# A hybrid decoder layer (gated linear attention and RWKV-7): one burst over four PSUM banks instead of two bursts over two

## The chip, the cores and the metric

The kernel runs on one core of one Trainium2 chip. The metric is device time in microseconds of one execution, the median of several. TensorE is written PE, VectorE DVE, ScalarE ACT, GpSimd POOL and SyncE, which starts the DMAs, SP.

## The reference

One layer is applied to 1024 prompt tokens and to 8 single sample tokens, in float32. The input is projected by `w_in` (1024 rows) to the columns of three groups: gated linear attention (GLA, 4 heads), RWKV-7 (16 heads of 64), and two gates. Both branches are recurrences over the tokens. The RWKV-7 one is, per head,

```python
def step(S, inp):
    rt, wt, kt, vt, kkt, at = inp
    sa = jnp.einsum('bhvk,bhk->bhv', S, -kkt)
    S = S * wt[:, :, None, :] + sa[..., None] * (kkt * at)[:, :, None, :] + vt[..., None] * kt[:, :, None, :]
    y = jnp.einsum('bhvk,bhk->bhv', S, rt)
    return S, y
...
m = (jax.nn.sigmoid(gate_a) * jnp.einsum('btc,cd->btd', o_gla, w_up_gla)
     + jax.nn.sigmoid(gate_b) * jnp.einsum('btc,cd->btd', o_rwkv, w_up_rwkv))
out = jnp.einsum('btd,de->bte', m, w_out)
y_out = _layernorm(DEEPNORM_ALPHA * x + out, ln_g, ln_b, LN_EPS)
```

The outputs are the layer's result for both groups of tokens and the new states.

## The kernel before

The prompt is worked on in two passes of 512 tokens (`PASS`, contexts `c` with `c.i` 0 and 1); the 8 sample tokens ride with the first. Everything is held with the channel on the 128 partitions and the token along the row. A weight block of 128 columns is projected by 24 matmuls a token tile (8 blocks of rows, and three products of high and low parts), in `blocks`; the two banks of tag `proj` take the results.

The RWKV-7 heads are worked on two at a time, head 0 on partitions 0 to 63 and head 1 on 64 to 127 (`HS`). So there are 8 pairs a pass, 16 in all; below they are counted 0 to 15 in order of time. A pair goes through these steps, each a generator that yields its instructions:

- `front`: decays and normalised keys; then the chunk matrices. The 512 tokens are `NCH` = 8 chunks of `C` = 64. The tile `BK` holds, for each chunk, the b and the k columns side by side (for head 1 in the order k, b: the slice begins at `h * C`), `AZ` the vectors that they are multiplied with. Two bursts of matmuls, for chunks 0 to 3 and 4 to 7, each over two PSUM banks (one a head), are masked by two multiplies each into `GG`. The diagonal blocks of `GG` go to DRAM (`LD`) and back, and 31 steps on DVE invert them (tile `X`, of which there is one buffer); the result goes over DRAM (`XD`) into `XT`.
- `back`: the off-diagonal blocks of the inverse.
- `turn`: transposes of the b and k rows of `BK` (16 transposes over two banks, copied back over `BK` itself), and of v.
- `chain`: the recurrence over the 8 chunks, three small matmuls each, one pair after the other (`self.chained`), in the bank of tag `pch`, with the outputs summed in the bank `pY`.
- `norm`: the norm over each head, bonus and gate.

The four GLA heads of a pass (`gla_head`), the low-rank projection (`low_rank`), the sample tokens and the loading of weights are further streams. PSUM has eight banks: 2 `proj`, 4 `big`, 1 `pch`, 1 `pY`. `BK`, `AZ`, `GG` and the tile `wide` have two buffers each, so two pairs are under way at most; rows of 512 or 520 tokens share 33 buffers (`row`).

The order of instructions is not written out. `Order.run` holds one pending instruction per stream, estimates when each could start, from costs and due times in the source, and issues the one with the earliest start less its stream's priority; the chip's engines then run their queues in that order. Buffers are given out in the same way: a stream that asks for `n` buffers of a tag goes on as soon as at least `n` are free, whoever else is waiting:

```python
        idle = self.idle[tag]
        if keep:
            yield lambda: len(idle) >= n + max(keep, self.wait[tag])
        elif len(idle) < n:
            self.wait[tag] += n
            yield lambda: len(idle) >= n
            self.wait[tag] -= n
```

`together` makes one entry of several PE instructions, so that nothing comes between them. `tr` is a transpose by the identity. `self.C.copy` is a copy on ACT or DVE, whichever is estimated to end first.

Of the kernel before, what the change touches and what calls it, by code (L numbers as in the profile page):

```python
# [20 lines left out]
P = 128  # L21
# [5 lines left out]
HT = TP // 2  # L27
# [5 lines left out]
C = 64  # L33
NCH = HT // C
# [54 lines left out]
HS = (slice(0, 64), slice(64, 128))  # L89
# [142 lines left out]
def together(ops):  # L232

    op = ops[0]
    fns = [x.fn for x in ops]
    op.ways = [(op.eng, lambda: [fn() for fn in fns], sum(x.cost for x in ops))]
    op.ins = [y for x in ops for y in x.ins]
    op.outs = [x.out for x in ops]
    op.eng, op.fn, op.cost = op.ways[0]
    return op  # L240
# [178 lines left out]
class Kern(Order):  # L419
# [679 lines left out]
    def front(self, c, p, st, d):  # L1099
        a, A, V, E = self.a, self.A, self.V, self.E  # L1100
        BK_, L_ = (yield from self.get("bk")), (yield from self.get("wide"))
        az, gg = (yield from self.get("az")), (yield from self.get("gg"))
        BK = BK_.rearrange("p (c t) -> p c t", c=NCH)
# [28 lines left out]
        ps = yield from self.head_sums(te)  # L1132
# [21 lines left out]
        ps = yield from self.head_sums(te)  # L1154
# [7 lines left out]
        H = NCH // 2  # L1162
        mk = self.cst("gmask").rearrange("p (k h t) -> p k h t", k=2, h=2)
        for x in range(0, NCH, H):
            ps = yield from self.get("big", 2)
            ps = [y.rearrange("p (c k t) -> p c k t", c=H, k=2) for y in ps]
            yield together([self.P.matmul(ps[h][:, n], BK[hs, x + n, h * C:h * C + P], AZ[hs, x + n], start=True, stop=True)
                            for n in range(H) for h, hs in enumerate(HS)])
            for h in range(2):
                yield V.tensor_mul(GG[:, x:x + H, :, h], ps[h], mk[:, :, h].unsqueeze(1).to_broadcast([P, H, 2, C]))  # L1170
            self.free(*ps)

        NU = 4 * NCH
        LD = self.dr.tile([4, NCH, 32, 32], F32, name=f"LD{c.i}{p}")
# [28 lines left out]
        H = NCH // 2  # L1203
# [4 lines left out]
        for q in range(2):  # L1208
            b = slice(32 * q, 32 * q + 32)
            for h in range(2):  # L1210
                n = 2 * q + h
# [31 lines left out]

    def turn(self, d):

        bt = d.BK.rearrange("p c t -> p (c t)")[:, :2 * HT].rearrange("p (c h k) -> p c h k", c=NCH, h=2)
        pt = yield from self.get("big", 2)
        yield together([self.tr(pt[h][:, x * C:x * C + C], d.BK[hs, x, h * C:h * C + P])
                        for x in range(NCH) for h, hs in enumerate(HS)])
        for h in range(2):  # L1250
            yield self.C.copy(bt[:, :, h], pt[h].rearrange("p (c k) -> p c k", k=C))
        self.free(*pt)
        d.bt = bt.rearrange("p c h k -> p c (h k)")
        d.u = d.L.rearrange("p (c h v) -> p c h v", c=NCH, h=2)
        pt = yield from self.bank("big", [P, 4, P])
        for n in range(4):
            yield self.tr(pt[:, n], d.v[:, n * P:(n + 1) * P])
        self.free(d.v)
        for h in range(2):
            for n, hs in enumerate(HS):  # L1260
                yield self.C.copy(d.u[HS[1 - h], n::2, h], pt[hs, :, h * C:h * C + C])
        self.free(pt)
# [534 lines left out]
```

## Time and profile before

| what | value |
|---|---|
| median of three runs | 1495.95 us (1495.26 to 1499.39) |
| the profiled execution, its own time | 1493.88 us |
| its span, first to last instruction | 1492.1 us |
| PE busy | 1466.4 us, 98% of the span |
| DVE busy | 1201.9 us, 81% |
| ACT busy | 880.1 us, 59% |
| granted TensorE clock, mean | 0.998 |

In the views a row names the engine, the operation, the tile written and the tiles read (`big<-az,bk`: a bank of tag big from `AZ` and `BK`), and the shape. For PE, `64*128` is the weights' rows and columns, the shape in which the array is used. A matmul of float32 operands is two instructions, a transpose one. The end of a matmul is modelled, and matmuls overlap, so what one costs is the step from its start to the next start, not its duration. All instructions stand at line 219, where the recorded calls are made, so that tiles tell more than lines.

### The profile page before, as it was taken

What the parts mean: (1) busy time and instruction counts of PE and PEld (TensorE: products, weight loads), DVE (VectorE), ACT (ScalarE), POOL (GpSimd) and SP (SyncE); (2) the same over time, 40 slices, a digit from 0 to 9 for tenths busy, and PEclk for the clock granted to TensorE, in tenths of its full rate; (3) what the DMA queues carried; (4) which work ended last, traced back from release to release, by engine and by line L of the source; (5) the groups of instructions that cost most, each with busy time, mean ns of one, the idle gap of its engine ahead of it and who ended that gap; (6) DMA issues with size and microseconds to landing.
All of it is one profiled execution on the core that took longest, in us unless ns stands there. A gap on an engine that the chain in (4) does not pass through costs nothing.

```text
span 1492.1 us, 30560 instructions
## 1 busy us (share of the span) xinstructions
PE 1466.4 (98%) x10678; PEld 1282.5 (86%) x10678; DVE 1201.9 (81%) x3159; ACT 880.1 (59%) x2221; POOL 115.5 (8%) x217
## 2 busy tenths in 40 slices
PE   9999999999999999999999999999999999999997
PEld 6998999999999999787877887787788899988786
DVE  6697889988998898979887998888777876756665
ACT  6665767767677677565754556465646746644210
POOL 1001002101120002001001010101000000000000
PEclk9999999999999999999999999999999999999999
DMA  9876697668767877675566565656554768887432
GB/s 310 282 267 207 221 314 227 218 220 302 234 220 221 297 239 241 185 237 168 165 203 175 161 199 180 181 154 171 177 172 135 234 197 258 282 300 264 143 106 85
DMA packets 211253, 319.01 MB, mean 214 GB/s; under 512 B 91683, under 2 KB 107180, under 8 KB 211100
## 3 DMA queue, kind: packets, MB, share of 16 engines
q1 hardware_dynamic: 211100, 317.06, 66.6%
q8 instruction: 85, 1.39, 0.4%
q14 instruction: 68, 0.56, 0.1%
HBM read 197.32 MB, written 118.61 MB: 212 GB/s over the span
## 4 chain that ended last, share of the span: by engine, by line
PE 83%; DVE 7%; DMA 4%; ACT 2%; issue 1%; SPq 1%; POOL 0%; POOLq 0%; DVEq 0%; ACTq 0%
PE proj L219 51%; PE big L219 22%; PE pch L219 6%; PE pY L219 5%; DVE row L219 2%; SPq L219 1%; DMA row<-o_rwkv 1%; ACT row L219 1%; DMA wraw<-w_in 1%; DVE X L219 1%; DVE wpart L219 1%; DMA wide<-LD 1%; DMA row<-state_rwkv 1%; DVE Xt L219 0%; ACT L397 0%
## 5 line engine op out<-in xcount | busy, mean ns | idle before, releaser
L219 PE MATMUL proj<-xs,wpart 128*128 128x264 f32 (+2 forms) x5640 | 1028.6, 327 | 1.2 <-DVE row L219 0.8
L219 PEld LDWEIGHTS proj<-xs,wpart 128*128 128x128 f32 x5640 | 814.4, 189 | 80.8 <-issue 10.3
L219 ACT CAST wpart<-wraw 128x512 fp32r<-128x512 f32 x210 | 130.2, 623 | 84.1 <-PE big L219 31.0
L219 DVE TENSOR_TENSOR wpart<-wraw,wpart 128x512 fp32r<-128x512 f32 x205 | 142.5, 697 | 33.4 <-ACT wpart L219 30.2
L219 DVE TENSOR_TENSOR row<-row 128x512 f32<-128x512 f32 (+10 forms) x295 | 156.8, 536 | 10.9 <-DMA row<-state_rwkv 6.2
L219 ACT ACTIVATE row<-row 128x512 f32<-128x512 f32 (+4 forms) x229 | 138.6, 610 | 26.2 <-DVE row L219 13.8
L219 POOL TENSOR_TENSOR row<-row 128x256 f32<-128x256 f32 (+7 forms) x74 | 70.3, 955 | 669.5 <-DVE row L219 232.9
L219 DVE TENSOR_TENSOR Xt<-X,wide 128x60 f32<-128x60 f32 (+24 forms) x496 | 108.4, 218 | 15.4 <-DMA wide<-LD 2.7
L219 DVE TENSOR_TENSOR X<-X,Xt 128x60 f32<-128x60 f32 (+24 forms) x496 | 106.0, 214 | 12.0
L219 ACT ACTIVATE row<-proj,omu 128x256 f32<-128x256 f32 (+1 forms) x99 | 54.3, 549 | 72.2 <-PE proj L219 71.8
L219 PE MATMUL big<-xs,wpart 128*128 128x512 f32 (+2 forms) x552 | 93.5, 324 | 0.0
L219 PEld LDWEIGHTS big<-xs,wpart 128*128 128x128 f32 x552 | 81.1, 188 | 8.7
L219 PE MATMUL big<-row 128*128 128x128 f32 (+4 forms) x464 | 86.6, 317 | 0.3 <-DVE Xt L219 0.3
L397 ACT ACT_TABLE_LOAD x64 | 82.1, 1283 | 1.1
L219 DVE SCALAR_TENSOR_TENSOR wide<-pch,pc,s0p 64x64 f32<-64x64 f32 x208 | 58.5, 281 | 28.3 <-PE pch L219 23.9
L219 DVE SCALAR_TENSOR_TENSOR row<-proj,pv,row 128x255 f32<-128x255 f32 (+1 forms) x99 | 56.3, 569 | 30.2 <-ACT tail L219 23.0
L219 ACT COPY row<-wide 64x64 f32<-64x64 f32 x240 | 57.9, 241 | 32.7 <-DVE wide L219 25.2
L219 ACT COPY wide<-pch 64x64 f32<-64x64 f32 x165 | 34.2, 207 | 65.1 <-PE pch L219 63.7
L219 PEld LDWEIGHTS big<-row 128*128 128x128 f32 (+3 forms) x464 | 60.5, 175 | 8.2 <-ACT row L219 0.8
L219 ACT COPY row<-big 128x128 f32<-128x128 f32 (+7 forms) x140 | 39.9, 313 | 41.7 <-PE big L219 40.4
L219 ACT ACTIVATE row<-proj 128x128 f32<-128x128 f32 (+4 forms) x136 | 36.9, 324 | 31.2 <-PE proj L219 30.5
L219 PE MATMUL big<-part,headsr 128*128 128x512 f32 x128 | 53.4, 418 | 1.7 <-DVE part L219 1.7
(234 smaller groups left out, 2025.8 us busy)
## 6 DMA issues: line engine op xcount, KB each, us to landing
w<-wpart SPq DMA_DIRECT2D x146, 512.0 KB
wpart<-w SPq DMA_DIRECT2D x146, 512.0 KB
wraw<-w_in SPq DMA_DIRECT2D x146, 256.0 KB
wide<-LD SPq DMA_DIRECT2D x64, 128.0 KB
wraw<-w_up_gla SPq DMA_DIRECT2D x32, 256.0 KB
wraw<-w_up_rwkv SPq DMA_DIRECT2D x32, 256.0 KB
sg<-row SPq DMA_DIRECT2D x16, 260.0 KB
row<-sg SPq DMA_DIRECT2D x16, 260.0 KB
```

Of the source, the lines that this page charges most:

```text
L219: ways.append((eng, lambda call=call: call(out, *args, **kw), price(eng, name, out, args, ins)))
L397: self.nc.scalar.preload_act_table_set(self.table)
```

## The change

The second burst of chunk matrices (chunks 4 to 7) asks for four banks of tag `big` instead of two. Behind its 8 products, in the same entry, stand the 16 transposes of the b and k rows of all 8 chunks, into the third and fourth bank. After the two masking multiplies the chunk banks are given back, the two copies bring the transposes back over `BK`, and the other two banks are given back; this stands ahead of the DMAs that write `LD`. `turn` begins with the transposes of v.

```diff
         for x in range(0, NCH, H):
-            ps = yield from self.get("big", 2)
-            ps = [y.rearrange("p (c k t) -> p c k t", c=H, k=2) for y in ps]
+            ps = yield from self.get("big", 2 if not x else 4)
+            turned = ps[2:]
+            ps = [y.rearrange("p (c k t) -> p c k t", c=H, k=2) for y in ps[:2]]
             yield together([self.P.matmul(ps[h][:, n], BK[hs, x + n, h * C:h * C + P], AZ[hs, x + n], start=True, stop=True)
-                            for n in range(H) for h, hs in enumerate(HS)])
+                            for n in range(H) for h, hs in enumerate(HS)]
+                           + [self.tr(turned[h][:, n * C:n * C + C], BK[hs, n, h * C:h * C + P])
+                              for n in range(NCH if turned else 0) for h, hs in enumerate(HS)])
             for h in range(2):
                 yield V.tensor_mul(GG[:, x:x + H, :, h], ps[h], mk[:, :, h].unsqueeze(1).to_broadcast([P, H, 2, C]))
             self.free(*ps)
+        bt = BK_[:, :2 * HT].rearrange("p (c h k) -> p c h k", c=NCH, h=2)
+        for h in range(2):
+            yield self.C.copy(bt[:, :, h], turned[h].rearrange("p (c k) -> p c k", k=C))
+        self.free(*turned)
+        d.bt = bt.rearrange("p c h k -> p c (h k)")
...
     def turn(self, d):
 
-        bt = d.BK.rearrange("p c t -> p (c t)")[:, :2 * HT].rearrange("p (c h k) -> p c h k", c=NCH, h=2)
-        pt = yield from self.get("big", 2)
-        yield together([self.tr(pt[h][:, x * C:x * C + C], d.BK[hs, x, h * C:h * C + P])
-                        for x in range(NCH) for h, hs in enumerate(HS)])
-        for h in range(2):
-            yield self.C.copy(bt[:, :, h], pt[h].rearrange("p (c k) -> p c k", k=C))
-        self.free(*pt)
-        d.bt = bt.rearrange("p c h k -> p c (h k)")
```

## The prediction

> **What bounds the kernel now.** I read the page's head first: busy shares, granted clock, the chain that ended last. Then the view of waits for PE alone.
>
> ```profile
> span 1492.1 us, 30560 instructions
> PE 1466.4 (98%) x10678; PEld 1282.5 (86%) x10678; DVE 1201.9 (81%) x3159; ACT 880.1 (59%) x2221; POOL 115.5 (8%) x217
> PEclk9999999999999999999999999999999999999999
> PE 83%; DVE 7%; DMA 4%; ACT 2%; issue 1%; SPq 1%; POOL 0%; POOLq 0%; DVEq 0%; ACTq 0%
> ...
> engine line waited for: us in total, times, longest us
> PE pch L219 <- DVE wide L219: 4.4, 6, 1.8
> PE pch L219 <- DVE rh L219: 2.5, 4, 1.0
> PE big L219 <- DMA X<-XD: 1.8, 1, 1.8
> ```
>
> TensorE has work in every slice, at full clock. Everything it waits for, the three rows here and thirteen smaller ones, comes to about 17.5 us in 1492. So the time is the number of PE instructions times their step, plus what the array loses between bursts. A change that moves latency of a pair gains nothing by that; a change that takes PE time out gains it in full, as long as the order of work still finds PE something to do.
>
> **The change part by part.** The matmuls concerned are grouped by the tile bk:
>
> ```profile
> L219 PE MATMUL big<-az,bk x512: 272/272/374, 58.4 to 1166.1; 64*128 64x128 f32 x171
> L219 PE MATMUL big<-cons,bk x256: 221/223/274, 130.8 to 1225.5; 64*128 64x64 f32 x128
> L219 ACT COPY bk<-big x25: 566/589/620, 131.6 to 1227.1; 128x512 f32<-128x512 f32 x25
> L219 DVE COPY bk<-big x7: 678/683/692, 633.0 to 1000.5; 128x512 f32<-128x512 f32 x7
> ```
>
> The 512 are the chunk matrices: 16 pairs, two bursts each, 16 instructions a burst. The 256 are the transposes: 16 pairs, one burst of 16. The 25 + 7 copies bring them back to SBUF, two a pair. None of these is removed. What goes is one burst as a separate thing: the transposes stop standing alone between 128x128 matmuls.
>
> *What a burst of transposes costs alone.* PE in order of time about pair 1's burst (start, duration, then the group; the views were asked with edges that cut the groups, so the same matmuls come back with other counts), and the mean of one neighbour:
>
> ```profile
> 187.57 0.53 PE L219 MATMUL proj<-xs,wpart 128*128 128x264 f32 x3
> 188.02 0.71 PE L219 MATMUL big<-cons,bk 64*128 64x64 f32 x16
> 188.67 0.39 PE L219 MATMUL proj<-xs,wpart 128*128 128x264 f32 x1
> 188.67 0.51 PE L219 MATMUL proj<-xs,wpart 128*128 128x264 f32 x2
> L219 PE MATMUL proj<-xs,wpart 128*128 128x264 f32 x1896 | 278.8, 290 | 0.0
> ```
>
> Three projections in a row take 0.53 us and one is on record with 0.29, so the step from one to the next is (0.53 - 0.29) / 2 = 0.12 us. The last of the three ends at 188.10, so it began at 187.81 and the next could have begun at 187.93. The transposes begin at 188.02: entry, 0.09. From there to the next projection 188.67 - 188.02 = 0.65. That projection is on record with 0.39 instead of 0.29: filling the array again, 0.10. Together 0.09 + 0.65 + 0.10 = 0.84 us of PE for one burst alone.
>
> *What the same transposes cost behind a chunk burst.* The second chunk burst of pair 8:
>
> ```profile
> 651.59 1.16 PE L219 MATMUL big<-az,bk 64*128 64x128 f32 x16
> 652.36 0.39 PE L219 MATMUL big<-az,bk 64*128 64x128 f32 x4
> 652.68 0.49 PE L219 MATMUL pch<-wide,bk 128*128 128x128 f32 x2
> ```
>
> The two heads run side by side, so the last four are two steps: 0.39 with one matmul at 0.27 leaves 0.12, about 0.11 a step. The last chunk matmul begins at 652.75 - 0.27 = 652.48 and the next work at 652.68, 0.20 later. With the transposes behind it, in the same 64-row, 128-column shape, the first begins one step later (0.11) and the next work 0.65 after that: 0.11 + 0.65 - 0.20 = 0.56 us added. The fill behind the burst is paid once, as now.
>
> So each pair saves 0.84 - 0.56 = 0.28 to 0.29 us, and 16 pairs 4.6 us.
>
> The one step without a row is the one from a chunk matmul to a transpose in this shape. From below it could cost nothing (the transpose slips in beside it: 0.39 a pair, 6.3 us in all). From above it could cost what leaving a chunk burst and filling again costs, 0.20 + 0.10 (0.10 a pair, 1.6 us). I take the step of the shape, 0.11, because shape and stationary operand stay what they are in the rows above.
>
> *The masking multiplies and the copies.* The two multiplies into gg need only the chunk banks, and a wait on PE counts up to the last matmul that wrote them, so they don't wait for the transposes. The two copies move from turn to front, count and cost as in the rows above, ACT or DVE as now; they stand ahead of the four DMAs that write LD, but those wait for gg from DVE, not for the copies. Price nothing, covered by the multiplies (0.68 us each). No DMA is added or removed; SP's queue gets the LD writes at the same place in the stream.
>
> *The four banks.* This is the step that can cost. All banks of tag big must be unused at one moment, and get with a count takes nothing until they are. A GLA head hands one bank on to itself from level 2 to its last chunk, and low_rank keeps one over the change of passes. Following takes and returns of that tag through the order in which before issues its work, against the times in the trace, the second burst would find four free banks this much later than now: pairs 0 to 7: 0, 20, 13, 23, 0, 28, 0, 58 us; pairs 8 to 15: 4, 9, 0, 2, 0, 3, 0, 0 us. The largest, pair 7:
>
> ```profile
> 572.09 1.05 PE L219 MATMUL big<-row,wa 128*16 128x512 f32 x8
> 576.06 1.27 PE L219 MATMUL big<-az,bk 64*128 64x128 f32 x16
> 577.98 2.53 SPq L219 DMA_DIRECT2D LD<-gg  x4
> 623.23 1.41 DVE L219 TENSOR_TENSOR row<-row,big 16x512 f32<-16x512 f32 x2
> 631.85 0.71 PE L219 MATMUL big<-cons,bk 64*128 64x64 f32 x16
> 637.81 0.27 PE L219 MATMUL pch<-wide,gg 128*128 128x128 f32 x1
> 677.06 1.15 PE L219 MATMUL pY<-gg,wide 128*64 128x64 f32 x32
> 717.67 1.16 PE L219 MATMUL big<-az,bk 64*128 64x128 f32 x16
> 792.80 1.16 PE L219 MATMUL big<-az,bk 64*128 64x128 f32 x16
> ```
>
> low_rank's bank is written from 572.09 and read to 624.6; then a head and pair 8's front hold one to about 634. Behind pair 7's second burst wait its LD writes, its solve (one buffer X, so pair 8's solve too), its turn and its chain (638 to 678), and, because bk and its like have two buffers, pair 9's front (717). By the distances in these rows the chain of pair 7 would run at about 695 to 735, pair 9's burst at about 745, and pair 10's, at 792.80 now, again in time. None of this is on PE's path: while pairs stand back, PE goes on with projections, gates and heads. I price it at nothing, with that cover named; it is gone if the row buffers run out, which is rival B. The delays of 13 to 28 us end before the pair two places on wants its buffers.
>
> *The wait for a bank.* The burst of 576.06 took 1.27 against 1.16 because the second bank came late; the worst of the sixteen, pair 3's, took 1.59, and the excess over all sixteen is about 1.3 us.
>
> ```profile
> 279.74 1.59 PE L219 MATMUL big<-az,bk 64*128 64x128 f32 x16
> ```
>
> With four banks, the ones free longest go to the chunk matmuls and the last to the transposes, 0.9 us later, which may hide it or, with four to wait for, double it: -1.3 to +1.3, taken as 0.
>
> [...] The rows have the burst's four banks read by two multiplies and two copies, and projections in their own two banks beside it. [...]
>
> **Sum.** The profiled execution took 1493.88 us, 1.8 of it around the span; minus 4.6 gives 1489.3. The median of the three runs shown is 2.1 above the profiled one, 1495.95, so I forecast 1491.3. Less than 0.3% (4.5 us) can't be told from no change here: the sum stands just at that edge.
>
> **The rivals.** *A, the gain is eaten by a new order.* The order of issue is worked out from costs; every later choice shifts with a burst. The waits of 17.5 us are what such an order leaves; a quarter more or less is 4 us. For it: the delays above change the order for half the kernel. Time about 1495, from 1492 to 1499.
>
> *B, row buffers run out.* Place: 700 to 780 us. Pair 7's chain and norm, some 55 us late, keep about four row buffers longer, and pair 9's front keeps its three inputs 26 us longer. Counting takes and returns, before is down to 3 of 33 free at 700 to 720, and to 1 at 560 to 580. At one free, the next projection can't begin and PE stands until a norm returns rows. Price: 5 to 12 us of idle PE, so about 1500. It decides when fewer than two rows are free for longer than a projection of one tile lasts (24 matmuls; by the first two rows here a step is (1.40 - 0.41) / 4 = 0.25 us, so 6 us). VectorE adds to it:
>
> ```profile
> 634.38 1.40 PE L219 MATMUL proj<-xs,wpart 128*128 128x512 f32 x5
> L219 PE MATMUL proj<-xs,wpart 128*128 128x512 f32 x1872 | 505.9, 406 | 0.0
> L219 DVE TENSOR_TENSOR Xt<-X,wide x31: 169/217/236, 592.9 to 616.2; 128x60 f32<-128x60 f32 x3, 128x28 f32<-128x28 f32 x2, 128x54 f32<-128x54 f32 x2, 128x48 f32<-128x48 f32 x2
> core 0: us, PE busy (x) PEld busy (x) DVE busy (x) ACT busy (x) POOL busy (x), PEclk, DMA share, GB/s
> 600.00:635.00 35.00, 34.72 (x240) 26.94 (x240) 31.65 (x94) 20.20 (x45) 1.70 (x6) 1.00 0.61 186
> 635.00:700.00 65.00, 64.97 (x392) 52.60 (x391) 55.77 (x171) 35.27 (x91) 1.40 (x2) 1.00 0.69 207
> ```
>
> A solve of 31 such operations and 31 additions behind them, 62 at some 0.21 us, 13 us, leaves the first stretch for the second, 55.8 of 65 busy already. Against it: pair 9's five working rows move out of the tight stretch with it.
>
> *C, more than the burst is saved.* Fewer waits for banks and a shorter turn: another 3 to 5 us of the 17.5, about 1487.
>
> *D, bubbles at the evacuation.* Each burst leaves all four banks to be read, 2 x 0.68 us on DVE and 2 x 0.59 on ACT; if PE stood for 1.4 us a pair, that is 22 us, about 1513. Against it: proj's banks. [...]
>
> **How the numbers follow.** The sum arrives, 1489.5 to 1493: 0.45, of which 0.26 is below 1491.5. A: 0.22. B: 0.12. C: 0.19. D: 0.02. Faster by over 0.3%: 0.26 + 0.19 = 0.45. Slower: B and D, less a part of B that stays within 4.5 us, 0.13. Same: 0.42. The range leaves out D, most of B and the end of C: 1486 to 1499; its lower end is also 6.3 from the bound of the step, with half of C.
>
> **What would show it.** Right: 16 groups of transposes directly behind 16 chunk matmuls, the next work about 1.85 us after the first of them; 16 fewer entries into the 64-row shape; mean durations as before. Pair 7's second burst near 634 and pair 9's near 745, pairs 10 to 15 where they are now. Wrong: the first transpose 0.2 us or more behind the last chunk matmul; PE waiting in proj for DVE or ACT at 560 to 580 or 700 to 780; waits for PE above some 21 us in sum.

## The result and the profile after

The changed kernel took 1514.09 us (median of four, 1513.47 to 1516.12) against 1497.38 us for before (median of four): ratio 1.0111, 95% interval 1.0093 to 1.0129. It is slower by 16.7 us, where 1491.3 was forecast, in a range of 1486 to 1499.

The page of the changed kernel, and its view of waits for PE:

```profile
span 1514.3 us, 30530 instructions
PE 1472.3 (97%) x10678; PEld 1287.8 (85%) x10678; DVE 1206.6 (80%) x3187; ACT 870.7 (57%) x2207; POOL 102.7 (7%) x193
PE   9999999999999997999999999999999999999997
PEclk9999999999999997999999999999999999999999
...
engine line waited for: us in total, times, longest us
PE pch L219 <- DVE wide L219: 9.9, 11, 1.9
PE big L219 <- DVE part L219: 3.4, 4, 1.8
PE big L219 <- DVE row L219: 3.2, 2, 2.8
PE big L219 <- DVE X L219: 3.2, 3, 1.9
```

There are as many PE instructions as before. Apart from the last slice, which ends at 7 tenths in both kernels, one of the 40 is short of work: the 16th, from 568 to 606 us, has PE and its clock at 7 tenths. The waits of PE are 33 us in sum against 17.5.

**The saving is there.** PE in order of time about pair 8's merged burst, in the changed kernel, and the group of the transposes:

```profile
678.91 1.16 PE L219 MATMUL big<-az,bk 64*128 64x128 f32 x16
679.90 0.66 PE L219 MATMUL big<-cons,bk 64*128 64x64 f32 x16
680.49 0.49 PE L219 MATMUL pch<-rh,XT 128*128 128x128 f32 x2
...
L219 PE MATMUL big<-cons,bk x256: 216/222/225, 63.4 to 1185.5; 64*128 64x64 f32 x128
```

The last chunk matmul ends at 680.07, lasts 0.27 and so began at 679.80; the first transpose begins 0.10 later, one step, with no further gap. From the first chunk matmul to the next work it is 680.49 - 678.91 = 1.58 us, against 652.68 - 651.59 = 1.09 before. In all 16 pairs of the changed kernel that distance is 1.58 or 1.59. The transposes add 0.49 where 0.56 was forecast, and by the prediction's rows their own burst had cost 0.84: 0.35 us a pair, an estimate of 5.6 us in all.

**The loss stands at the change of passes.** Stretches of before, then of the changed kernel (columns: stretch, its length, busy time with number of instructions for PE, PEld, DVE, ACT and POOL, granted clock, DMA share, GB/s):

```profile
560.00:575.00 15.00, 15.00 (x127) 13.53 (x126) 14.27 (x33) 11.83 (x31) 5.01 (x6) 1.00 0.83 294
575.00:600.00 25.00, 25.00 (x203) 23.05 (x202) 21.36 (x61) 16.72 (x47) 4.63 (x12) 1.00 0.70 206
600.00:625.00 25.00, 25.00 (x172) 20.20 (x172) 22.37 (x75) 13.51 (x30) 1.02 (x5) 1.00 0.55 168
```

```profile
560.00:575.00 15.00, 14.08 (x157) 12.56 (x156) 14.44 (x49) 8.20 (x21) 1.43 (x2) 1.00 0.55 184
575.00:600.00 25.00, 16.13 (x83) 12.83 (x84) 21.40 (x56) 14.04 (x31) 1.50 (x4) 0.59 0.24 56
600.00:625.00 25.00, 25.00 (x191) 20.99 (x191) 21.54 (x47) 18.52 (x51) 1.02 (x7) 1.00 0.43 143
```

From 575 to 600 us PE ran 83 matmuls instead of 203. It had nothing to do for 25 - 16.13 = 8.9 us, and the granted clock was 0.59. The clock was at half rate from 576.8 to 597.3 us; that stretch, and the 3.4 us before it:

```profile
576.81:597.29 20.48, 12.49 (x55) 9.48 (x56) 18.70 (x44) 12.38 (x26) 1.50 (x4) 0.50 0.22 54
573.40:576.81 3.41, 1.65 (x11) 1.15 (x10) 3.31 (x14) 0.80 (x2) 0.00 (x0) 1.00 0.84 184
```

Only the 12.5 us in which PE was busy can have been lengthened by the half rate, so it cost some 6 us at most (an estimate: half of 12.5). PE's own list shows what it did there (start, time from first start to last end, tile and operands, count):

```profile
576.28 0.48 PE L219 MATMUL big<-part,headsr 128*128 128x512 f32 x1
...
578.68 1.19 PE L219 MATMUL big<-row 128*128 128x128 f32 x4 [1.92 <-ACT row L219]
579.52 1.20 PE L219 MATMUL big<-lw,l2p 128*128 128x512 f32 x2
...
583.50 1.22 PE L219 MATMUL big<-part,headsr 128*128 128x512 f32 x2
...
587.48 1.19 PE L219 MATMUL big<-row 128*128 128x128 f32 x4 [2.75 <-DVE row L219]
590.56 0.65 PE L219 MATMUL big<-X,L 128*32 128x128 f32 x8 [1.89 <-DVE X L219]
```

There is no projection between 574 and 594 us: what is left are small matmuls that wait for each other through DVE and ACT, and two of 512 columns take 1.20 us, where two of that kind took 0.62 in before (at 544.67 us): the half clock. What sets the fall off is not shown: in the 3.4 us before it PE was busy for 1.65, and its longest idle stretch there was 1.71 us. The longest of all, 2.75 us, came when the clock was already low.

**How it came to that.** The first and second burst of pair 5, the end of its chain (pY) and the first matmul of pair 7's front (lw,l2p), in before; then the same in the changed kernel, with pair 7's two bursts behind them:

```profile
422.74 1.16 PE L219 MATMUL big<-az,bk 64*128 64x128 f32 x16
...
425.07 1.16 PE L219 MATMUL big<-az,bk 64*128 64x128 f32 x16
...
520.49 1.15 PE L219 MATMUL pY<-gg,wide 128*64 128x64 f32 x32
...
542.64 0.39 PE L219 MATMUL big<-lw,l2p 128*128 128x512 f32 x1
```

```profile
449.89 1.16 PE L219 MATMUL big<-az,bk 64*128 64x128 f32 x16
...
465.69 1.16 PE L219 MATMUL big<-az,bk 64*128 64x128 f32 x16
...
567.96 1.15 PE L219 MATMUL pY<-gg,wide 128*64 128x64 f32 x32
...
579.52 1.20 PE L219 MATMUL big<-lw,l2p 128*128 128x512 f32 x2
...
611.28 1.16 PE L219 MATMUL big<-az,bk 64*128 64x128 f32 x16
...
622.94 1.16 PE L219 MATMUL big<-az,bk 64*128 64x128 f32 x16
```

Pair 5's second burst stands 15.8 us behind its first instead of 2.3, but the first is late too, by 27 us: the waits of pairs 1 and 3, whose second bursts stand 18.5 and 13.3 us behind their first, have been handed on. Pair 5's chain ends 47 us late, and pair 7's front, which needs that pair's buffers, begins 37 us late. The rest is not in a view: it comes from following the order of issue through the kernel's source, set against the times of the trace. The front had its tiles at 568 us instead of 541, and then asked for five row buffers when three were free. Of the thirty in use, 15 held projected rows of pairs and GLA heads and five held rows of x for pass 1; gates and running work held the others. While the front waits, the rule of `get` leaves no row to a new projection. It had its five at 578, and then none was free: the next projections stand at 594.65.

### The profile page after: what moved, and what is told of

Read it like the earlier page. It is cut to its first block, busy times and chain, and to the rows that moved or that the text cites. A ratio compares the mean times of both kernels' runs of the same rounds, so it can differ in the third digit from the quotient of the medians.

```text
span 1514.3 us, 30530 instructions
## 1 busy us (share of the span) xinstructions
PE 1472.3 (97%) x10678; PEld 1287.8 (85%) x10678; DVE 1206.6 (80%) x3187; ACT 870.7 (57%) x2207; POOL 102.7 (7%) x193
## 5 line engine op out<-in xcount | busy, mean ns | idle before, releaser
L219 DVE TENSOR_TENSOR row<-row 128x256 f32<-128x256 f32 (+8 forms) x313 | 159.7, 516 | 7.2 <-ACT row L219 3.1
L219 DVE TENSOR_TENSOR Xt<-X,wide 128x60 f32<-128x60 f32 (+24 forms) x496 | 108.1, 218 | 22.4 <-DMA wide<-LD 11.6
L219 DVE TENSOR_TENSOR X<-X,Xt 128x60 f32<-128x60 f32 (+24 forms) x496 | 110.0, 222 | 11.7
L219 POOL TENSOR_TENSOR row<-row 128x512 f32<-128x512 f32 (+6 forms) x56 | 58.9, 1054 | 842.3 <-DVE row L219 267.6
L219 PEld LDWEIGHTS pch<-wide,gg 128*128 128x128 f32 x256 | 42.6, 189 | 20.0 <-PE proj L219 7.9
```

The lines of the kernel that those rows point to most:

```text
L219: ways.append((eng, lambda call=call: call(out, *args, **kw), price(eng, name, out, args, ins)))
```

## The experiments

Theory 1: the demand for four free banks makes fronts late, and the row buffers run out at the change of passes. Rival 2: the order of before is a lucky one, and any change of it costs some 10 us. Rival 3: the early transposes and copies themselves hold pairs up.

**The parts of the change one by one.** First the transposes moved but not merged:

```diff
+        turned = yield from self.get("big", 2)
+        yield together([self.tr(turned[h][:, n * C:n * C + C], BK[hs, n, h * C:h * C + P])
+                        for n in range(NCH) for h, hs in enumerate(HS)])
+        bt = BK_[:, :2 * HT].rearrange("p (c h k) -> p c h k", c=NCH, h=2)
...
```

> The transposes and their copies stand in front, right behind the second chunk burst, but as a burst of their own over two banks: moved as in the change, not merged, and nothing waits for four banks. Theory 1 (the demand for four free banks makes fronts late, until the row buffers run out at the change of passes and TensorE stands idle): no such demand, so no standstill at 570 to 600 us and a time of 1492 to 1500. Rival 2 (the order of work of before is a lucky one, and any change of it costs some 10 us): 1503 to 1513. Rival 3 (the early transposes and copies themselves hold pairs up): 1508 or more.

1498.54 us, ratio 1.0013 (1.0001 to 1.0026). Rival 3 falls: moved by themselves the transposes cost 1.4 us. But a small standstill came with them, and no wait for four banks: from 575 to 600 us the granted clock was 0.86 and PE ran 179 matmuls.

Then the wait alone, in before:

```diff
+            if x and len(self.idle["big"]) < 4:
+                self.wait["big"] += 4
+                yield lambda: len(self.idle["big"]) >= 4
+                self.wait["big"] -= 4
             ps = yield from self.get("big", 2)
```

> The kernel before, in which the second chunk burst is held until four banks of tag big are free, and then takes two as before; the transposes stay in turn. Theory 1: the loss of the change without its gain, 1514 + 4.6 = about 1518, with TensorE idle for several us about the change of passes and pair 7's front some 30 us late. Rival 2: like any other order, 1503 to 1513. Rival 3: no transposes are moved, so 1492 to 1500.

1524.68 us, ratio 1.0185 (1.0159 to 1.0212): the wait without the gain costs more than the change. Its stretch from 575 to 600 is the one above again:

```profile
575.00:600.00 25.00, 17.17 (x103) 10.93 (x104) 23.03 (x49) 17.09 (x34) 4.87 (x9) 0.59 0.21 55
```

The merge without the wait (`turn` keeps its own burst where no banks were free):

```diff
-            ps = yield from self.get("big", 2 if not x else 4)
+            ps = yield from self.get("big", 4 if x and len(self.idle["big"]) == 4 else 2)
```

> The merged burst only where four banks of tag big are free when the second burst asks; otherwise the burst takes two and the transposes stay in turn. In the order of before that is so for 7 of 16 pairs. Theory 1: nothing waits, 7 x 0.29 = 2 us saved, 1491 to 1497. Rival 2: 1503 to 1513. Rival 3: about half of the change's loss, 1500 to 1506.

1501.76 us, ratio 1.0035 (1.0019 to 1.0051): a miss for theory 1 and rival 2; it lies in the range of rival 3, which had already fallen. In its own order five pairs merged, not seven. PE ran 203 matmuls at full clock from 575 to 600 us, and yet the kernel was 4.6 us slower, which made rival 2 worth its own runs.

More row buffers in the changed kernel (`"row"` 33 to 35):

> The changed kernel with 35 row buffers instead of 33. Theory 1 with row buffers as the last link: the standstill at 570 to 600 us gets much shorter, the time falls by 8 to 20 us, to 1494 to 1506. If late fronts cost by themselves, or by rivals 2 and 3, it stays at 1510 to 1516.

1509.43 us, ratio 1.0102 (1.0063 to 1.0141), short of the forecast. The standstill shrank as it should (first row), and pair 7's front began 2.8 us behind pair 5's chain instead of 11.6. But PE lost time again from 600 to 650, 4.0 us of it in one wait of a small matmul for DVE, and then pair 8's second burst stood 33 us behind its first:

```profile
575.00:600.00 25.00, 22.97 (x140) 18.71 (x140) 22.93 (x52) 15.86 (x31) 3.95 (x4) 0.93 0.63 192
600.00:650.00 50.00, 45.65 (x321) 38.11 (x320) 31.90 (x80) 29.14 (x79) 5.61 (x11) 0.93 0.45 131
```

**The order by itself.** Two neutral orders of before, a cost and a priority nudged (`SPARE` 0.4 to 0.41; `"turn"` 0.5 to 0.51):

> The kernel before with nothing changed but one cost in the order's estimates (SPARE 0.41 instead of 0.4): the same instructions in another order. Rival 2 (the order of before is a lucky one, so that any other loses about 10 us): 1503 to 1512. Theory 1 alone (orders without the four-bank wait are alike): 1493 to 1501.

> The kernel before with the priority of turn at 0.51 instead of 0.5: a second neutral order. Same expectations as for the first: rival 2 says 1503 to 1512, theory 1 alone 1493 to 1501. The two together measure what a change of order is worth by itself.

1512.74 us, ratio 1.0113 (1.0092 to 1.0133), and 1505.80 us, ratio 1.0068 (1.0051 to 1.0086). Both are as rival 2 said, the first just above its range: the same work in another order cost 9 and 16 us. That this is so for any order is not shown, as the moved transposes cost 1.4. The changed kernel in another order (`"head"` 0.3 to 0.31), and the merge if free with `SPARE` 0.41:

> The changed kernel with the priority of the GLA heads at 0.31 instead of 0.3. In this order the second bursts of pairs 1 and 4 come after 48 and 21 matmuls instead of 121 and 83, and the row buffers run short less often. Theory 1 (the wait for four banks and the row buffers behind it): a shorter standstill at the change of passes, 1496 to 1507. If the merged burst costs by itself, or late fronts cost wherever they are: 1510 to 1518.

> The kernel that merges only where four banks are free, with SPARE at 0.41: another order of the same idea. Theory 1 (no wait, 0.29 us saved for each merged pair) with orders that differ by some 5 us: 1488 to 1498, perhaps below before. Rival 2: 1503 or more.

1497.29 us, ratio 1.0004 (0.9993 to 1.0014), and 1499.76 us, ratio 1.0037 (1.0012 to 1.0063), the second between its two forecasts. In the first the four-bank waits are still there, pair 7's 31 us long. Pair 5's chain ended at 545 us, 25 later than in before, but pair 7's front began right behind it, at 547 instead of 543, and nothing stood still:

```profile
580.94 1.16 PE L219 MATMUL big<-az,bk 64*128 64x128 f32 x16
...
612.01 1.16 PE L219 MATMUL big<-az,bk 64*128 64x128 f32 x16
...
575.00:600.00 25.00, 25.00 (x194) 21.10 (x193) 19.39 (x41) 16.98 (x46) 2.08 (x7) 1.00 0.96 337
```

So a long wait behind the first burst was harmless at that place. Where over 20 us were lost, the front was late: it began at 560 to 585 us in the changed kernel, in the wait alone and in the merge of pass 0, and with `SPARE` 0.41 and `"turn"` 0.51. The partners of these orders, with and without the change, and the fast one with 35 rows:

> The changed kernel with SPARE at 0.41: the partner of the neutral order that took 1512.7 without the change. If the change itself costs through the wait for four banks (theory 1), it adds 8 to 20 us to that order: 1520 to 1532. If the loss is the order's alone (rival 2), both changes of order draw from the same lot: 1497 to 1514.

> The changed kernel with the priority of turn at 0.51: the partner of the neutral order that took 1505.8 without the change. Theory 1: 1513 to 1525. Rival 2: 1497 to 1514.

> The kernel before with the priority of the GLA heads at 0.31: the partner of the changed kernel that took 1497.3 with it. Theory 1: without the wait this order is 8 to 17 us better than its partner, 1481 to 1490, or at least not worse. Rival 2: a neutral order like the other two, 1502 to 1512, so slower than its partner.

> The changed kernel with the heads at 0.31 and 35 row buffers. If what is left of the loss there (some 5 us between 560 and 1180 us) is row buffers, 1490 to 1496 and so below before; if it is the waits of the order, 1495 to 1505.

1522.23 us, ratio 1.0181 (1.0152 to 1.0210); 1513.18, ratio 1.0120 (1.0092 to 1.0148); 1505.93, ratio 1.0070 (1.0045 to 1.0095); 1493.82, ratio 0.9983 (0.9968 to 0.9998). The first is in theory 1's range alone, the second in the ranges of both; the partner of the fast order came out as rival 2 said.

**Both causes apart.** The end of PE's work in each profile can be set against before's, and the lag split into what it gains between its projections 3360 and 3600 (561.9 and 626.3 us in before, the change of passes) and the rest. The times are medians, the lags those of the one profiled execution, and before's was a short one, at 1493.88 us:

| order | without the change: time; at the change of passes; elsewhere | with it |
|---|---|---|
| of before | 1497.4; 0; 0 | 1514.1; +22.0; -0.7 |
| SPARE 0.41 | 1512.7; +10.2; +11.3 | 1522.2; +22.1; +6.8 |
| turn 0.51 | 1505.8; +1.4; +8.5 | 1513.2; +21.3; +1.3 |
| head 0.31 | 1505.9; -3.1; +16.8 | 1497.3; -6.0; +10.5 |

Elsewhere the change is 0.7, 4.5, 7.2 and 6.3 us better than its partner, 4.7 on average. That is near the saving of 5.6, but the split is coarse: between the two projections the changed kernel ran some 100 matmuls of other kinds more than before, so a part of its 22 us there is work moved and not time lost, and elsewhere looks better by as much. At the change of passes three of four orders with it lose 21 to 22 us, and without it the four stand between -3 and +10. The wait alone lost 25.6 there, the changed kernel with 35 rows 8.4, and the transposes moved by themselves 7.4. So an order can lose some 10 us at that place without any wait for four banks. The last runs merge in one pass only, and the other pass keeps the burst in `turn` (shown for pass 0; `c.i == 1` for pass 1):

```diff
-            ps = yield from self.get("big", 2 if not x else 4)
+            ps = yield from self.get("big", 4 if x and c.i == 0 else 2)
```

> The merged burst over four banks for the pairs of pass 0 alone; in pass 1 two banks, and the transposes in turn. Theory 1 (waits for four banks in pass 0 make pair 7's front late, the row buffers run out at the change of passes, TensorE stands and its clock drops): pass 0 is as in the changed kernel, the standstill of 21 to 26 us stays, 1510 to 1521. Rival 2 (only the order of before is lost): 1502 to 1510, with no standstill at the change of passes.

> The merged burst for the pairs of pass 1 alone. Theory 1: pass 0 runs in the order of before up to pair 8, no standstill, 8 x 0.29 = 2.3 us saved, and a new order from 650 us on that may cost up to some 8 us: 1494 to 1503. If the merged burst itself cost: 1503 to 1508.

> The same with the priority of the GLA heads at 0.31, the partner of the neutral order of 1505.9. Theory 1: 1505.9 less 2.3 us, 1498 to 1506, as the order from pair 8 on is new; rival 2: 1502 to 1512.

> The merge in pass 1 alone with 35 row buffers and SPARE at 0.42: a trial for a version that beats both kernels. By theory 1 there is no standstill, and what is left is the order's luck: 1490 to 1500; below 1493 it would beat before.

Pass 0 alone: 1510.39 us, ratio 1.0101 (1.0077 to 1.0125), with 22.0 us lost at the change of passes. Pass 1 alone: 1500.01, ratio 1.0027 (1.0009 to 1.0044), with 0.5 lost there. Pass 1 alone, head 0.31: 1495.67, ratio 1.0005 (0.9991 to 1.0019), below the forecast. Pass 1 alone, 35 rows, SPARE 0.42: 1493.46, ratio 0.9986 (0.9973 to 1.0000). The first two in the stretch from 575 to 600:

```profile
575.00:600.00 25.00, 16.96 (x89) 13.63 (x90) 21.33 (x54) 14.38 (x31) 1.50 (x4) 0.59 0.18 46
```

```profile
575.00:600.00 25.00, 24.96 (x201) 22.91 (x201) 21.03 (x60) 16.54 (x45) 4.62 (x12) 1.00 0.66 209
```

The merge in pass 0 alone makes the standstill, the clock's fall with it; that in pass 1 makes none. With the wait alone and the 35 rows this shows the cause of the loss: the demand for four banks in pass 0, through a late front and the row buffers. It needs the order as well, as head 0.31 has the demand and no standstill. The last kernel of the four and the changed one with head 0.31 and 35 rows are 2 to 3 us below before, at the edge of their intervals; as an order alone is worth more than that, it isn't shown that the merge did it.

## Why the prediction was wrong

- *The saving per burst* held, by the step of 0.10 us between chunk matmul and transpose. Its size was low: 0.35 us a pair instead of 0.28 to 0.29, because the transposes add 0.49 us and not 0.56. The 1.85 us that the prediction names as a sign doesn't follow from its own sum, which gives 1.09 + 0.56 = 1.65; it is 1.58.
- *The four banks* is the step that failed. The waits were foreseen one by one, and priced at nothing because "the delays of 13 to 28 us end before the pair two places on wants its buffers". That was read off the pairs' bursts, but a front takes its tiles some 30 us before its burst: pair 7's at 541 in before, with its burst at 573.5. So there was no such slack, and the delays of pairs 1, 3 and 5 added up: pair 5's chain ended 47 us late, and in the changed kernel that led to the standstill. Pair 7's own 58 us, which looked the worst, came to about 9, since low_rank was nearly done when the late front arrived.
- *PE goes on with projections* held up to the change of passes and failed there, where the row buffers were gone. Of the signs of being wrong that the prediction named, its waits came true: 33 us against 21. Rival B had the mechanism. It named 560 to 580 us as the tightest place, at one free buffer of 33, and then put the standstill at 700 to 780. Its price of 5 to 12 us covers the idle time of 8.9 us and leaves out the clock, some 6 us at most.
- *Rival A's* size, a quarter of the 17.5 us of waits, was too small. Three neutral orders cost 8.5 to 16.8 us elsewhere than at the change of passes, and before lies below all three. Its 1495.95 is not what a changed kernel of this kind starts from; about 1505, the mean of the four orders without the change, is nearer.
- *Rival D* didn't come about: in all 16 pairs the next work begins 1.58 or 1.59 us after the first chunk matmul, so nothing waits there while the four banks are read.
- *The copies and multiplies* at no cost: the run with the transposes moved and not merged bears it out, 1.4 us. The masking multiplies don't wait for the transposes, as the prediction argued: pair 7's first begins at 624.13 us, right behind its last chunk matmul, while its transposes go on to 624.60.

## What to carry to other kernels

A demand for all buffers of a kind at one moment is a wait for the slowest of their other users: price it by the place where the delayed work next takes a buffer, not by where its visible burst stands, and add the delays of successive items up. Where the order of a kernel comes from a greedy planner, measure a few neutral orders first: a gain of some microseconds can't be read from one pair of kernels when the order alone can be worth 9 to 16. And when TensorE starves, count the clock with the idle time: here 8.9 us of idle PE and a granted clock of 0.59 stood in the same 25 us.

## What the runs showed of the hardware

In the changed kernel the granted clock fell to half at 576.8 us, after 3.4 us of which PE was busy for 1.65 and in which its longest idle stretch was 1.71, and it stayed down for 20.5 us, of which PE was busy for 12.5. Two other stretches at half rate in that run, from 160.4 and from 1266.3 us, lasted 3.4 us each. In the wait alone and the merge of pass 0 the granted clock from 575 to 600 us was 0.59 on average, as in the changed kernel; the longest single wait of PE was 2.8 us in the changed kernel, 2.5 in the wait alone and 2.8 in the merge of pass 0. A burst of 16 transposes alone between 128*128 matmuls cost some 0.84 us of PE (pair 1 of before, by the prediction's rows); behind a burst of its own shape it added 0.49 (pair 8, 1.58 in the changed kernel against 1.09 in before), 0.35 less, and the first transpose followed after a step of 0.10.
